# Smaller first loads, more warming products and a halved last store in a two-layer encoder trunk

## The chip, the cores and the metric

The kernel runs on one core of one Trainium2 chip. The metric is device time in microseconds (us), the median of several runs. All work is in float32, carried by the tensor engine in its float32r form (high and low parts, see below). Engine names are those of the profile: PE is the tensor engine's product, PEld its weight load, DVE the vector engine, ACT the scalar engine, POOL GpSimd, SP the sync engine. A small q behind a name is that engine's instruction queue, where its loads and stores are issued.

## What is computed

Two layers of one encoder trunk over 256 tokens of 2048 channels. Cut to what matters here:

```python
def hybrid_layer(x, cos, sin, norm_g, w_in, ...):
    h = rmsnorm(x, norm_g)
    proj = h @ w_in                      # 2048 x 13376
    (c_a, c_glu, c_gate, q_down, kv_down, k_pe, m_gate, g_conv, g_mla) = split(proj)
    y_conv = conv_branch(c_a, c_glu, c_gate, ...) @ w_proj_conv
    y_mla = mla_branch(q_down, kv_down, k_pe, m_gate, cos, sin, ...) @ w_proj_mla
    y = sigmoid(g_conv) * y_conv + sigmoid(g_mla) * y_mla
    return x + y @ w_out

def reference(x, positions, ...):
    cos, sin = rope_tables(positions, x.dtype)
    for l in range(2):
        x = hybrid_layer(x, cos, sin, ...)
    return x
```

## The kernel before

**The stream of weights.** All weights are cut into blocks of at most 512 columns, a block into pieces of four K tiles (a K tile is 128 rows of the weight), and a piece into two splits of two K tiles. `load` brings a piece into one of three `raw` buffers with one load on SP's queue. `split` makes the high part `hi` on ACT (L175) and the low part `lo` on DVE (L176), into one of three buffers each. `product` then runs, for each split, each half t of the tokens and each of the split's K tiles, three products into one accumulator: high by `hi` (L211), high by `lo` (L212), low by `hi` (L213). That is 12 products in a split and 96 in a block of 16 K tiles. Splits are asked for two ahead of the products, loads two pieces ahead. Four accumulators `acc` make two blocks; a block's accumulators must be evacuated before the block after next begins.

**The order.** A scheduler orders each engine's instructions by a simulated timeline; the priority is the order of the program. An instruction passed to `keep_in_program_order` is held behind the instruction that was traced last on its engine before it.

**The start.** Block 0 is the first of three blocks of the down projections (384, 384 and 320 columns). Its stationary operands are the transposed input times the norm's gain, split as well: `h_hi` on ACT (L326) and `h_lo` on DVE (L327), 16 K tiles of 256 tokens each. `x_in` is loaded in chunks of 2, 2, 4, 4 and 4 K tiles on SP, with the first pieces of weights between them; piece 0 is loaded in two halves. Ahead of these SP loads the `gains`. While the loads are on their way nine products of zeros (L258) run on PE. The constants of the rotary tables, `invf` (one row, broadcast to all partitions) and `pos`, are loaded on POOL's queue, and some 60 small DVE instructions (L275 to L303) and four Sin on ACT make the tables from them. `load_consts` loads two sets of constants on SP during block 1.

**The norm's factor.** `first_sums` loads the untransposed input in eight parts on SP (L333), ACT sums their squares (L335), and `sum_x` makes `rinv_x` from them on DVE. `down_evac` (L362) needs it to evacuate block 0.

**The end.** `wout_evac` adds an accumulator to the residual (L759) and, in the last layer, stores the 128x512 result on SP's queue (L761), 256 KB each. The last block's two halves of tokens are the last two of these.

Of the kernel before, what the change touches and what calls it, by code (L numbers as in the profile page):

```python
# [11 lines left out]
F32 = mybir.dt.float32  # L12
# [7 lines left out]
P = 128  # L20
T = 2
SEQ = 256
D = 2048
NCT = D // P
DEPTH = 2
# [15 lines left out]

# Columns of the input projection, by part.
O_A, O_GLU, O_CGATE = 0, D, 2 * D
# [4 lines left out]

# Widths of the blocks that the down projections are cut into.
DOWN_BLOCKS = ((0, 384), (384, 384), (768, 320))  # L50

# Per-partition constants of a layer: where each begins.
C_CB, C_LG, C_LB, C_QG, C_KG, C_CW = 0, 16, 32, 48, 49, 50
C_N = C_CW + NCT * CONV_W
R_QA, R_KVA, R_QR, R_KR, R_N = 0, LORA, 2 * LORA, 2 * LORA + ROPE, 2 * LORA + 2 * ROPE

KG = 4  # K tiles in one load of weights
KS = 2  # K tiles in one split of weights
N_WARM = 9  # products of zeros that warm the tensor engine's clock
SUMS_AFTER = 1  # splits before the loads for the first sums of squares  # L60

# [3 lines left out]
def revolution_pieces():  # L65
    """1 / (2 pi) as a sum of 12-bit pieces, each exact in float32."""
    from fractions import Fraction

    pi = Fraction(
        "3.14159265358979323846264338327950288419716939937510582097494459230781640628620899"  # L70
    )
    rest, out = 1 / (2 * pi), []
    for i in range(REVOLUTION_PIECES):
        unit = Fraction(1, 1 << (12 * (i + 1)))
        n = int(rest / unit)
        out.append(float(n * unit))
        rest -= n * unit
    return out


def blocks_of_layer():
    """(stream, K tiles, columns) of each block of a layer, in each stream's order."""
    s = {"win": [], "wuq": [], "wukv": [], "wpc": [], "wpm": [], "wo": []}
    for _, n in DOWN_BLOCKS:
        s["win"].append(n)
    s["win"] += [512] * 24
    s["wuq"] = [2 * QK] * NPAIR
    s["wukv"] = [2 * (NOPE + VH)] * NPAIR
    for w in ("wpc", "wpm", "wo"):
        s[w] = [512] * 4  # L90
    return s
# [3 lines left out]
def trunk(ctx: ExitStack, tc: tile.TileContext, xT, x, g_in, pos, win, wuq, wukv, wpc, wpm, wo, cst, rows, invf, out):  # L95
    nc = tc.nc
    pool = lambda name, bufs, **kw: ctx.enter_context(tc.tile_pool(name=name, bufs=bufs, **kw))
    const = pool("const", 1)
# [15 lines left out]

# [1 line left out]
    streams = {"win": (win, 16), "wuq": (wuq, 4), "wukv": (wukv, 4), "wpc": (wpc, 16), "wpm": (wpm, 16), "wo": (wo, 16)}  # L116
# [17 lines left out]

# [1 line left out]
    plans = []  # L136
# [17 lines left out]
    def load(i):  # L154
        if i >= len(pieces) or i in loaded:
            return
        ap, n = pieces[i]
        t = raw_p.tile([P, KG, n], F32, tag="raw", name=f"raw{i}")
        step = KS if i == 0 else KG
        for k in range(0, KG, step):  # L160
            if i == 0:
                load_x(k // step)
            nc.sync.dma_start(t[:, k : k + step, :], ap[:, k : k + step, :])
        loaded[i] = t

    def split(i):
        if i >= len(splits) or i in done:
            return
        piece, h, n = splits[i]
        load(piece)  # L170
        r = loaded[piece][:, h * KS : (h + 1) * KS, :]
        hi = split_p.tile([P, KS, n], F32R, tag="hi", name=f"hi{i}")
        lo = split_p.tile([P, KS, n], F32R, tag="lo", name=f"lo{i}")
        with tc.high_priority(offset=SPLIT_SOONER):
            nc.scalar.copy(hi, r)  # L175
            nc.vector.tensor_sub(lo, r, hi.bitcast(F32))  # L176
        done[i] = hi, lo
        for a in range(1, LOAD_AHEAD + 1):
            load(piece + a)

# [1 line left out]
    attn, fill = deque(), deque()  # L182
# [39 lines left out]

# [1 line left out]
    def rsqrt(y, ms):  # L224
        """y = ms ** -0.5, both float32 views of the same shape."""
        shape = list(ms.shape)
# [14 lines left out]

# [1 line left out]
    ident = const.tile([P, P], F32, name="ident")  # L243
    make_identity(nc, ident)
    ones = const.tile([P, P], F32, name="ones")
    nc.vector.memset(ones, 1.0 / D)

    cos2 = const.tile([P, T, 2, HALF], F32, name="cos2")
    sin2 = const.tile([P, T, 2, HALF], F32, name="sin2")

    # The engines' first steps while the first loads are on their way: the tensor engine's clock
    # and the table of the activations.
    zeros = work.tile([P, 512], F32R, tag="junk", name="zeros")
    nc.vector.memset(zeros.bitcast(F32), 0.0)
    nc.scalar.copy(sin2[:, 0, 0, :], ones[:, :HALF])
    warm = tp_p.tile([P, 512], F32, tag="tp", name="warm")
    for i in range(N_WARM):
        nc.tensor.matmul(warm, zeros[:, :P], zeros, start=i == 0, stop=i == N_WARM - 1)  # L258

    gains = const.tile([P, DEPTH, NCT], F32, name="gains")  # L260
    nc.sync.dma_start(gains, g_in)
    x_in = big.tile([P, NCT, SEQ], F32, tag="big", name="x_in")
    x_chunks = [(0, 2), (2, 4), (4, 8), (8, 12), (12, 16)]

    def load_x(i):
        a, b = x_chunks[i]
        nc.sync.dma_start(x_in[:, a:b, :], xT[:, a:b, :])

    def rope_tables():
        invf_t = const.tile([P, HALF], F32, name="invf_t")  # L270
        nc.gpsimd.dma_start(invf_t, invf.partition_broadcast(P))
        pos_t = const.tile([P, T], I32, name="pos_t")
        nc.gpsimd.dma_start(pos_t, pos)
        posf = const.tile([P, T], F32, name="posf")
# [13 lines left out]
        def reduce_to(dst, src, scale):  # L288
            """dst = src * scale less the nearest whole number (src * scale is exact)."""
            nc.vector.tensor_scalar(whole, src, scale, big_half, op0=ALU.mult, op1=ALU.add)  # L290
            nc.vector.tensor_scalar(whole, whole, -big_half, None, op0=ALU.add)
            nc.vector.scalar_tensor_tensor(dst, src, scale, whole, op0=ALU.mult, op1=ALU.subtract)
# [21 lines left out]

# [1 line left out]
    h_hi = big.tile([P, NCT, SEQ], F32R, tag="big", name="h_hi")  # L316
    h_lo = big.tile([P, NCT, SEQ], F32R, tag="big", name="h_lo")
    load(0)
    for i in range(2, len(x_chunks)):
        load_x(i)  # L320
        if i < len(x_chunks) - 1:
            load(i - 1)
    consts = [const.tile([P, C_N], F32, name=f"cst{l}") for l in range(DEPTH)]
# [12 lines left out]

# [1 line left out]
    for l in range(DEPTH):  # L338
# [3 lines left out]

        # -- down projections --
        down_row = big.tile([P, T * DOWN + R_N], F32, tag="big", name=f"down{l}")
# [19 lines left out]
        def down_after(down=down, qkc=qkc, ss_d=ss_d, r_d=r_d, kpe=kpe, ccq=ccq, ssq_t=ssq_t, gqk=gqk, row=row, C=C):  # L364
# [24 lines left out]

            # The shared rotary key, gained and rotated.  # L390
            gained(ccq, cos2, R_KR)
# [11 lines left out]

        # -- attention --
        # Transposed queries and keys of a pair of heads: the parts without a rotary key (high and low
        # of q, of k), then the rotary parts, where head 0 has [q high; q low], [k high; k high] and
        # [k low; 0] on the two halves of the partitions and head 1 the halves swapped.
        qk_t = big.tile([P, 14 * SEQ], F32R, tag="big", name=f"qk_t{l}")
# [46 lines left out]
        def attention(b, pair_of=pair_of, ss_d=ss_d, kpe=kpe, ccq=ccq, ssq_t=ssq_t, gqk=gqk, nope_t=nope_t, rope_t=rope_t, rope_k=rope_k, rope_l=rope_l, o_sb=o_sb, pt_h=pt_h, pt_l=pt_l, rinv=rinv):  # L455
# [56 lines left out]
            def scores():  # L512
                s0 = s_p.tile([P, 2, 2, P], F32, tag="s0", name="s0")
                s1 = s_p.tile([P, 2, SEQ], F32, tag="s1", name="s1")
                # The first block of queries: the keys' high and low parts side by side.
                for h in range(2):
# [19 lines left out]
                for s, nkeys in ((s0, P), (s1, SEQ)):  # L536
                    # The first chunk of a block of queries doesn't see the block's second chunk of keys.
                    nc.vector.memset(s[:CHUNK, :, nkeys - CHUNK :], MASKED)
# [53 lines left out]

        # -- convolution --
        us, vs = {}, {}
# [89 lines left out]

        # -- gates, projections, output --
        keep = {}

        def four(evac_src, dst_hi, dst_lo, c, t):
            """Turn a [tokens, 512 channels] tile and split it into the stationary operand's parts."""
            tp = tp_p.tile([P, 4, P], F32, tag="tp", name="tp4")  # L690
# [64 lines left out]
        def wout_evac(c, t, ps, keep=keep, l=l, last_layer=last_layer):  # L755
            blk = slice(c * 512, (c + 1) * 512)
            xt = wide_p.tile([P, 512], F32, tag="w", name="xres")
            nc.gpsimd.dma_start(xt, (x if l == 0 else x1_dram)[t, :, blk])
            nc.vector.tensor_add(xt, ps, xt)  # L759
            if last_layer:  # L760
                nc.sync.dma_start(out[t, :, blk], xt)  # L761
                return
# [17 lines left out]

        # -- run --
        for kind, i, pl in planned:
# [51 lines left out]

# [1 line left out]
def _blocked(w, widths):  # L836
    """[K, N] -> per block of columns: [K / 512][128][4][columns], flat."""
    k, at, out = w.shape[0] // (KG * P), 0, []
    for n in widths:
        b = w[:, at : at + n].reshape(k, KG, P, n).transpose(0, 2, 1, 3)  # L840
        out.append(b.reshape(-1))
        at += n
    return np.concatenate(out)
# [60 lines left out]
```

## Time and profile before

| | us |
|---|---|
| median of 3 runs | 1961.72 |
| lowest and highest of the 3 | 1961.68 to 1962.62 |
| span of the profiled execution | 1960.8 |
| PE busy in the span | 1951.5 |
| DVE busy | 1546.2 |
| ACT busy | 1107.4 |

The median of the runs stands 0.92 us above the span of the profiled execution, which runs from its first to its last instruction. Busy times are shares of the span; several engines are busy at the same time. Products are pipelined, so the duration of one is longer than the distance from one to the next.

### The profile page before, as it was taken

The page shows a single profiled execution, that of the slowest core. Times are in us where ns is not written, and L with a number is a line of the kernel's source. Part 1 is how long each engine was busy: PE and PEld are TensorE (multiplying, and loading weights), DVE is VectorE, ACT ScalarE, POOL GpSimd, SP SyncE. Part 2 cuts the span into 40 slices and gives each one's busy share as a digit, 9 for nine tenths or more (in the row PEclk, how much of TensorE's full clock was granted, in tenths as well). Part 3 has the DMA queues.
Part 4 walks back from the last instruction along what each step waited for, and adds up shares of the span by engine and source line. Part 5 has one row for each costly group of instructions (what it writes and reads, how often), then busy time and mean ns, then how long its engine had stood idle before and what let it go on. Part 6 is the DMA issues. An engine that isn't in the chain of part 4 may idle for free.

```text
span 1960.8 us, 25239 instructions
## 1 busy us (share of the span) xinstructions
PE 1951.5 (100%) x9333; PEld 1649.7 (84%) x9333; DVE 1546.2 (79%) x2738; ACT 1107.4 (56%) x1761; POOL 17.6 (1%) x50
## 2 busy tenths in 40 slices
PE   9999999999999999999999999999999999999999
PEld 8888888888888888888898888888888888888887
DVE  7788987889998787555557888878899987875554
ACT  6668767665443456444556686676654434464443
POOL 0000000000000000000000000000000000000000
PEclk9999999999999999999999999999999999999999
DMA  7654444445555555456665544444455555554564
GB/s 287 209 178 160 172 164 160 164 169 177 195 194 191 194 187 193 178 197 216 204 217 187 186 154 166 176 150 170 170 182 192 197 192 194 186 188 177 199 225 150
DMA packets 55532, 365.17 MB, mean 186 GB/s; under 512 B 6496, under 2 KB 6512, under 8 KB 16496
## 3 DMA queue, kind: packets, MB, share of 16 engines
q1 hardware_dynamic: 53424, 357.25, 51.7%
q0 software_dynamic: 1984, 6.31, 0.9%
q8 instruction: 73, 1.20, 0.2%
q14 instruction: 51, 0.42, 0.1%
HBM read 359.34 MB, written 4.19 MB: 185 GB/s over the span
## 4 chain that ended last, share of the span: by engine, by line
PE 98%; DVE 1%; DMA 0%; ACT 0%; issue 0%; SPq 0%
PE acc L212 31%; PE acc L213 31%; PE acc L211 31%; PE o_ps L580 1%; PE s L534 1%; PE tp_qk L489 1%; DVE v_t L670 0%; PE tp_rope L502 0%; PE tp_mg L706 0%; PE tp L692 0%; PE tp_u L607 0%; DMA raw<-in_win 0%; PE tp_cg L735 0%; DVE lo L176 0%; PE s L520 0%; PE s L518 0%
## 5 line engine op out<-in xcount | busy, mean ns | idle before, releaser
L175 ACT CAST hi<-raw 128x1024 fp32r<-128x1024 f32 (+2 forms) x688 | 704.9, 1025 | 747.9 <-PE acc L213 508.9
L176 DVE TENSOR_TENSOR lo<-raw,hi 128x1024 fp32r<-128x1024 f32 (+2 forms) x688 | 816.0, 1188 | 324.2 <-ACT hi L175 321.1
L627 DVE SCALAR_TENSOR_TENSOR v_t<-u_t,cst,v_t 128x256 f32<-128x256 f32 x960 | 412.3, 478 | 1.1
L212 PE MATMUL acc<-lo,h_hi 128*128 128x512 f32 (+2 forms) x864 | 334.0, 387 | 0.2 <-DVE lo L176 0.2
L212 PE MATMUL acc<-lo,hT 128*128 128x512 f32 (+2 forms) x864 | 333.2, 386 | 0.2 <-DVE lo L176 0.2
L213 PE MATMUL acc<-hi,h_lo 128*128 128x512 f32 (+2 forms) x864 | 332.8, 385 | 0.0
L213 PE MATMUL acc<-hi,hT 128*128 128x512 f32 (+2 forms) x864 | 332.1, 385 | 0.0
L211 PE MATMUL acc<-hi,h_hi 128*128 128x512 f32 (+2 forms) x864 | 305.3, 386 | 2.9 <-ACT hi L175 2.9
L211 PE MATMUL acc<-hi,hT 128*128 128x512 f32 (+2 forms) x864 | 303.8, 384 | 0.0
L211 PEld LDWEIGHTS acc<-hi,h_hi 128*128 128x128 f32 x864 | 162.1, 189 | 32.9 <-ACT hi L175 3.6
L212 PEld LDWEIGHTS acc<-lo,h_hi 128*128 128x128 f32 x864 | 163.0, 189 | 30.0 <-DVE lo L176 1.3
L212 PEld LDWEIGHTS acc<-lo,hT 128*128 128x128 f32 x864 | 162.3, 188 | 29.5 <-DVE lo L176 0.8
L213 PEld LDWEIGHTS acc<-hi,h_lo 128*128 128x128 f32 x864 | 162.9, 189 | 28.5
L213 PEld LDWEIGHTS acc<-hi,hT 128*128 128x128 f32 x864 | 162.3, 188 | 28.5
L211 PEld LDWEIGHTS acc<-hi,hT 128*128 128x128 f32 x864 | 161.4, 188 | 29.5
L212 PE MATMUL acc<-lo,ycT 128*128 128x512 f32 x256 | 100.5, 392 | 0.0
L212 PE MATMUL acc<-lo,yT 128*128 128x512 f32 x256 | 99.9, 390 | 0.0
L213 PE MATMUL acc<-hi,ycT 128*128 128x512 f32 x256 | 99.9, 390 | 0.0
L213 PE MATMUL acc<-hi,yT 128*128 128x512 f32 x256 | 99.7, 389 | 0.0
L213 PE MATMUL acc<-hi,oT 128*128 128x512 f32 x256 | 99.6, 389 | 0.0
L212 PE MATMUL acc<-lo,oT 128*128 128x512 f32 x256 | 99.6, 389 | 0.0
L212 PE MATMUL acc<-lo,qkc 128*128 128x384 f32 (+1 forms) x256 | 94.2, 368 | 0.0
(207 smaller groups left out, 2270.5 us busy)
## 6 DMA issues: line engine op xcount, KB each, us to landing
raw<-in_win SPq DMA_DIRECT2D x192, 1024.0 KB, 4.8
raw<-in_wpm SPq DMA_DIRECT2D x32, 1024.0 KB, 4.8
raw<-in_wpc SPq DMA_DIRECT2D x32, 1024.0 KB, 4.7
raw<-in_wo SPq DMA_DIRECT2D x32, 1024.0 KB, 4.9
raw<-in_wukv SPq DMA_DIRECT2D x16, 1024.0 KB, 4.8
raw<-in_wuq SPq DMA_DIRECT2D x16, 768.0 KB, 4.2
raw<-in_win SPq DMA_DIRECT2D x15, 768.0 KB, 5.7
raw<-in_win SPq DMA_DIRECT2D x8, 640.0 KB, 3.9
```

The lines of the kernel that those rows point to most:

```text
L175: nc.scalar.copy(hi, r)
L176: nc.vector.tensor_sub(lo, r, hi.bitcast(F32))
L211: nc.tensor.matmul(pts[t][:, :n], sh, hi[:, kk, :], start=first, stop=False)
L212: nc.tensor.matmul(pts[t][:, :n], sh, lo[:, kk, :], start=False, stop=False)
L213: nc.tensor.matmul(pts[t][:, :n], sl, hi[:, kk, :], start=False, stop=last)
L489: nc.tensor.transpose(tp[:, h, t * P : (t + 1) * P], src[:, t, h, :NOPE], ident)
L534: nc.tensor.matmul(s1[:, h, :], qa, ka, start=n == 0, stop=n == len(terms) - 1)
L580: nc.tensor.matmul(o_ps[:, h, kt * P :], v[j][:, kt, h, :], pt[i][:, h, queries], start=n == 0, stop=n == len(todo) - 1,)
L627: nc.vector.scalar_tensor_tensor(dst, src, w, dst, op0=ALU.mult, op1=ALU.add)
```

## The change

Five edits, all at the start or the end of the program:

- Piece 0 is loaded in steps of 1, 1 and 2 K tiles, and the chunks of `x_in` become 1, 1, 2, 4, 4 and 4 K tiles, one chunk before each step. Split 0 is made K tile by K tile.
- The `gains` are loaded on ACT's queue instead of ahead of `x_in` on SP's.
- Eleven warming products instead of nine, and DVE clears `zeros` before it fills `ones`.
- `invf` and `pos` are loaded on SP's queue and held behind the load that was traced last there (piece 6), no longer on POOL's. The tables' arithmetic is the same.
- In the last block of columns of the last layer each 128x512 sum and store become two of 128x256, one stored on SP's queue, one on ACT's.

Comments and docstrings are left out too. The core of the diff:

```diff
-N_WARM = 9  # products of zeros that warm the tensor engine's clock
+FIRST_STEPS = ((0, 1), (1, 2), (2, 4))
+N_WARM = 11
...
-        step = KS if i == 0 else KG
-        for k in range(0, KG, step):
+        for j, (a, b) in enumerate(FIRST_STEPS if i == 0 else ((0, KG),)):
             if i == 0:
-                load_x(k // step)
-            nc.sync.dma_start(t[:, k : k + step, :], ap[:, k : k + step, :])
+                load_x(j)
+            nc.sync.dma_start(t[:, a:b, :], ap[:, a:b, :])
...
+        step = 1 if i == 0 else KS
         with tc.high_priority(offset=SPLIT_SOONER):
-            nc.scalar.copy(hi, r)
-            nc.vector.tensor_sub(lo, r, hi.bitcast(F32))
+            for a in range(0, KS, step):
+                s = slice(a, a + step)
+                nc.scalar.copy(hi[:, s], r[:, s])
+                nc.vector.tensor_sub(lo[:, s], r[:, s], hi[:, s].bitcast(F32))
...
-    nc.vector.memset(ones, 1.0 / D)
...
+    x_chunks = [(0, 1), (1, 2), (2, 4), (4, 8), (8, 12), (12, 16)]
...
+    nc.scalar.dma_start(gains, g_in)
     zeros = work.tile([P, 512], F32R, tag="junk", name="zeros")
     nc.vector.memset(zeros.bitcast(F32), 0.0)
+    nc.vector.memset(ones, 1.0 / D)
...
-    nc.sync.dma_start(gains, g_in)
...
-        nc.gpsimd.dma_start(invf_t, invf.partition_broadcast(P))
+        tc.keep_in_program_order(nc.sync.dma_start(invf_t, invf.partition_broadcast(P)))
         pos_t = const.tile([P, T], I32, name="pos_t")
-        nc.gpsimd.dma_start(pos_t, pos)
+        tc.keep_in_program_order(nc.sync.dma_start(pos_t, pos))
...
-    for i in range(2, len(x_chunks)):
+    for i in range(3, len(x_chunks)):
         load_x(i)
         if i < len(x_chunks) - 1:
-            load(i - 1)
+            load(i - 2)
...
-            nc.vector.tensor_add(xt, ps, xt)
+            last = last_layer and c == 3
+            for a, engine in ((0, nc.sync), (256, nc.scalar)) if last else ():
+                s = slice(a, a + 256)
+                nc.vector.tensor_add(xt[:, s], ps[:, s], xt[:, s])
+                engine.dma_start(out[t, :, c * 512 + a : c * 512 + a + 256], xt[:, s])
+            if not last:
+                nc.vector.tensor_add(xt, ps, xt)
             if last_layer:
-                nc.sync.dma_start(out[t, :, blk], xt)
+                if c < 3:
+                    nc.sync.dma_start(out[t, :, blk], xt)
                 return
```

## Rows read from the trace of the kernel before

**Rows 1.** The page's first line.

```profile
span 1960.8 us, 25239 instructions
```

**Rows 2.** Timeline of the start: start, duration, engine, instruction, idle before.

```profile
0.74 0.39 SPq L261 DMA_DIRECT2D gains<-in_g  x1
...
0.83 0.17 DVE L246 MEMSET ones<- 128x128 f32 x1 [0.83 <-PEq L893]
1.05 0.48 DVE L254 MEMSET zeros<- 128x512 f32 x1
1.18 0.42 SPq L267 DMA_DIRECT2D x_in<-in_xT  x1
1.28 0.67 POOL L271 DMA_DIRECT2D invf_t<-in_invf  x1 [0.34 <-issue]
...
1.59 4.21 PE L258 MATMUL warm<-zeros 128*128 128x512 f32 x9 [1.59 <-DVE zeros L254]
...
3.54 0.43 SPq L163 DMA_DIRECT2D raw<-in_win  x1
...
7.97 0.17 DVE L275 CAST posf<-pos_t 128x2 f32<-128x2 int32 x1 [2.16 <-DMA pos_t<-in_pos]
```

**Rows 3.** The chain that ended last, its pieces at the start: start, length, what.

```profile
8.67 1.01 PE acc L211 x2
...
12.91 0.32 PE acc L213
...
13.84 0.17 PE acc L212
```

**Rows 4.** Busy time by stretch; the last two columns are DMA share and GB/s.

```profile
3.50:6.50 3.00, 2.30 (x6) 1.29 (x4) 0.88 (x2) 0.91 (x2) 0.34 (x5) 1.00 0.62 117
6.50:12.50 6.00, 3.83 (x11) 3.34 (x12) 4.02 (x13) 4.18 (x8) 0.00 (x0) 1.00 1.04 419
```

**Rows 5.** DMA issues: tile, queue, size, us from issue to landing (raw: piece 1).

```profile
gains<-in_g SPq DMA_DIRECT2D x1, 16.0 KB, 1.6
invf_t<-in_invf POOLq DMA_DIRECT2D x1, 16.0 KB, 5.4
...
x_in<-in_xT SPq DMA_DIRECT2D x1, 256.0 KB, 3.1
...
raw<-in_win SPq DMA_DIRECT2D x1, 768.0 KB, 9.1
...
out<-xres SPq DMA_DIRECT2D x2, 256.0 KB, 2.3
```

**Rows 6.** Groups by shape, first 60 us: busy, mean ns of one, idle before.

```profile
L176 DVE TENSOR_TENSOR lo<-raw,hi 128x768 fp32r<-128x768 f32 x16 | 15.3, 955 | 2.4 <-ACT hi L175 2.3
L175 ACT CAST hi<-raw 128x768 fp32r<-128x768 f32 x16 | 13.1, 831 | 8.4 <-PE acc L213 4.4 <-DMA raw<-in_win 2.7 <-DVE whole L291 1.2
...
L176 DVE TENSOR_TENSOR lo<-raw,hi 128x640 fp32r<-128x640 f32 x8 | 6.6, 825 | 6.7 <-ACT hi L175 6.7
L175 ACT CAST hi<-raw 128x640 fp32r<-128x640 f32 x8 | 5.8, 728 | 5.6 <-PE acc L213 5.6
...
L291 DVE TENSOR_SCALAR whole<-whole 128x64 f32<-128x64 f32 x14 | 2.7, 193 | 0.2
```

**Rows 7.** Timeline around the rotary tables, block 0's evacuation and block 2's start.

```profile
24.47 0.42 SPq L163 DMA_DIRECT2D raw<-in_win  x1
...
26.88 0.96 DVE L176 TENSOR_TENSOR lo<-raw,hi 128x768 fp32r<-128x768 f32 x1 [0.87 <-ACT hi L175]
...
42.42 0.16 DVE L235 SCALAR_TENSOR_TENSOR rinv_x<-rsq_t,rinv_x 128x2 f32<-128x2 f32 x1
...
43.28 1.51 ACT L362 ACTIVATE down<-acc,rinv_x 128x384 f32<-128x384 f32 x3
...
44.53 0.31 PE L211 MATMUL acc<-hi,h_hi 128*128 128x320 f32 x1
```

**Rows 8.** Timeline of the end.

```profile
1956.39 0.69 DVE L759 TENSOR_TENSOR xres<-acc,xres 128x512 f32<-128x512 f32 x1 [0.44 <-PE acc L213]
```

More of the change, by code (lines that the diff above doesn't have):

```diff
@@ L245, in trunk, with load_x @@
     ones = const.tile([P, P], F32, name="ones")
-    nc.vector.memset(ones, 1.0 / D)
     cos2 = const.tile([P, T, 2, HALF], F32, name="cos2")
     sin2 = const.tile([P, T, 2, HALF], F32, name="sin2")
+    x_in = big.tile([P, NCT, SEQ], F32, tag="big", name="x_in")
+    x_chunks = [(0, 1), (1, 2), (2, 4), (4, 8), (8, 12), (12, 16)]
+    def load_x(i):
+        a, b = x_chunks[i]
+        nc.sync.dma_start(x_in[:, a:b, :], xT[:, a:b, :])
+    gains = const.tile([P, DEPTH, NCT], F32, name="gains")
+    nc.scalar.dma_start(gains, g_in)
     zeros = work.tile([P, 512], F32R, tag="junk", name="zeros")
     nc.vector.memset(zeros.bitcast(F32), 0.0)
+    nc.vector.memset(ones, 1.0 / D)
     nc.scalar.copy(sin2[:, 0, 0, :], ones[:, :HALF])
@@ L258, in trunk @@
         nc.tensor.matmul(warm, zeros[:, :P], zeros, start=i == 0, stop=i == N_WARM - 1)
-    gains = const.tile([P, DEPTH, NCT], F32, name="gains")
-    nc.sync.dma_start(gains, g_in)
[L262 to L267, printed above, removed]
     def rope_tables():
         invf_t = const.tile([P, HALF], F32, name="invf_t")
-        nc.gpsimd.dma_start(invf_t, invf.partition_broadcast(P))
+        tc.keep_in_program_order(nc.sync.dma_start(invf_t, invf.partition_broadcast(P)))
         pos_t = const.tile([P, T], I32, name="pos_t")
-        nc.gpsimd.dma_start(pos_t, pos)
+        tc.keep_in_program_order(nc.sync.dma_start(pos_t, pos))
         posf = const.tile([P, T], F32, name="posf")
```

## The prediction

> **What bounds the kernel now.** I read the page first. Its span is 1960.8 us [rows 1], and the table above gives PE 1951.5 us of it. Only 9.3 us remain in which PE doesn't run, so whatever the change can win lies there, or in products at less than full speed. The list of waits and the chain show where they are. At the start PE first waits for the zeros, runs nine warming products to 1.59 + 4.21 = 5.80, and then stands still until 8.67 [rows 2, 3]. From there the chain is PE products one behind another to the end, so a start that is earlier by some time, or faster, is an end that is earlier by that much, as long as nothing else comes to hold PE.
>
> The pieces of the chain also show a clock. The products of 384 columns follow one another by 0.32 us up to 13.8 and by 0.17 from there [rows 3]: 1.2 columns a nanosecond is the lower of the tensor engine's two levels (1.2 GHz), 2.2 is the upper one (2.4 GHz). The clock column reads 1.00 in both stretches [rows 4], so here the distances tell more than the column. From 8.67 to 13.84 there are 14 products at the lower level. From 13.84 to the first product of block 2 at 44.53 there are 2 x 96 - 14 = 178, that is 0.1724 us each [rows 3, 7]: no waits are hidden in them. I therefore write PE's progress as the time at which it would have started had it run at full speed throughout: 13.84 - 14 x 0.1724 = **11.43 us**. The kernel's gain at the start is 11.43 less the same figure of the changed kernel.
>
> At the end, the last sum starts on DVE at 1956.39 and takes 0.69 [rows 8]; the store that follows lands 2.3 us after its issue [rows 5].
>
> **Start: three limits, the latest decides.**
>
> *Warming.* DVE clears zeros first instead of second, so they are ready 1.05 - 0.83 = 0.22 us sooner (the second clearing starts where the first did). The warming products then start at 1.37. Two more of 512 columns at 1.2 per ns cost 0.85, so they end at 1.37 + 4.21 + 0.85 = 6.43 [rows 2]. PE works in order, so no real product starts before about 6.4, however early the data are.
>
> *Clock.* In the trace the rise came 5.0 us after products were resumed at 8.67, and the nine before the idle time brought none. If the run is unbroken from 1.37, the same 5.0 us give 6.4: no real product at the lower level. The bounds are no product and again 14 products at the lower level, which cost 14 x (0.32 - 0.1724) = 2.07 us. I take 0, since idle time is what separates the two runs of products in the trace. The Trainium skill, TensorE: Matmul & The Clock Gate (The HAM clock gate), says that the lower level is the default, that activity lifts it, and that the number of products at it varies between runs of one kernel. That agrees with the 14 here; its variation no run here shows.
>
> *Data.* K tiles 0 and 1 come early: x's first load moves from 1.18 to 0.74, where the gains stood [rows 2]. Split 0 in two parts costs more: from 768 to 640 columns ACT saves 0.103 and DVE 0.130 us [rows 6], so 384 columns cost 0.831 - 0.309 = 0.52 on ACT and 0.955 - 0.390 = 0.565 on DVE, twice each, or 0.21 and 0.18 more than whole. The warming products cover this; without them it would add at most 0.4. The load that is late next is piece 1, which holds K tiles 4 to 7 whole and feeds split 2. It was issued at 3.54 and landed 9.1 us later, at 12.64 [rows 2, 5]. From x's first issue at 1.18 that is 11.46 us. K tiles 0 to 7 of x and weights are 2.62 MB, 6.26 us at the 419 GB/s of the next stretch [rows 4]; 5.20 us are something else. Between 3.5 and 6.5 the rate was only 117 GB/s, worth 3.0 x (1 - 117/419) = 2.16 us [rows 4]. That is when POOL's two loads were in flight: the 16 KB of invf took 5.4 us from 1.28, where the 16 KB of the gains took 1.6 on SP [rows 2, 5]. I read the first as crowding out the weights. The change takes both from the start, so 2.16 goes and 3.04 is left. The fixed part of a lone load is between 1.6 (gains) and 3.04; I take 2.3. Two more loads ahead of piece 1 cost between nothing and two issues, which follow one another by (3.54 - 1.18) / 5 = 0.47 [rows 2]; I take 0.4. Piece 1 then lands at 0.74 + 6.26 + 2.3 + 0.4 = 9.7 (bounds 0.74 + 6.26 + 1.6 = 8.6, and 12.2 if nothing but the earlier issue counts). With hi (0.83) and lo (0.955) behind it and 0.04 between, lo of split 2 is there at 11.55. The 26th product is the first to need it: 11.55 - 25 x 0.1724 = **7.24**. That is later than 6.43, so the data decide.
>
> The gain at the start is 11.43 - 7.24 = **4.19 us**. The bounds are 11.43 - 6.43 = 5.0 (data in time) and, with piece 1 at 12.2, 11.43 - (14.04 - 4.31) = 1.7.
>
> A rule speaks against the small loads: the Trainium skill, DMA: Bandwidth & Descriptors (Rules for kernel authors, and its fit in Anatomy of one DMA), wants 1 MiB a load and gives 2.0 us fixed per load plus bytes at 436 GB/s. By it 128 KB would take an estimated 2.3 us against 2.6 for 256 KB, and two more loads paid in turn would eat 4 us, leaving no gain. The trace's loads overlap: they are issued 0.47 us apart and land together at 419 GB/s, so I give the rule a small share, under the third rival.
>
> **Rotary tables.** Their two loads move from POOL's queue to SP's, behind piece 6 at 24.47 [rows 7], by then some 4.2 us earlier. What is queued behind them on SP, the two sets of constants and the next pieces, moves back by two issues of about 0.42. lo of split 9 starts at 26.88 [rows 7], PE comes to it at 11.43 + 108 x 0.1724 = 30.05, so 2.2 us of slack cover this. The DVE work of some 60 x 0.2 = 12 us [rows 6] leaves the first 20 us, which helps split 2, and falls after it; their first use that PE comes to is after block 2. I cost it at nothing.
>
> **Block 0's evacuation.** It starts at 43.28, three in 1.51 us, so the first ends at 43.8; block 2 wants that accumulator at 44.53 [rows 7]. The slack is 0.7. With PE 4.2 earlier, rinv_x must come 3.5 earlier. The squares before it stand between ACT's splits, which PE paces, so I expect them to move along; nothing is taken off, 3.5 us is the price if they don't.
>
> **End.** A half sum costs 0.69 - 256 x 0.00102 (DVE's slope above) = 0.43; two cost 0.86. The last store is issued 0.17 later and carries 128 KB less, 0.31 us at 419 GB/s: **0.14 us** gained. Bounds: 0.31 gained (halves at half price) and 0.38 lost (halves at full price).
>
> **Sum.** 4.19 + 0.14 = 4.33 us: a span of 1956.5. The median of the runs stands 0.92 above the span, so 1961.72 - 4.33 = **1957.4 us**. A measurement of this kernel can tell about 0.2%, 3.9 us, from no change: the bar is 1957.8.
>
> **The rivals.**
>
> 1. *The data are no limit* (chance 0.18). Piece 1 lands by 8.9, PE starts at 6.43 and never waits: 5.0 + 0.14, 1956.6. For it: the 16 KB of the gains landed in 1.6. Against it: 3.04 us of the first loads' time have no explanation but a slow beginning.
> 2. *The clock doesn't rise in the warming* (0.08). Fourteen products at 1.2 GHz from 6.43 give 8.5: 2.9 + 0.14, 1958.7. For it: nine products of zeros raised nothing.
> 3. *The loads stay slow at the start* (0.10). Then POOL's loads weren't the cause, or the small loads eat what they freed: 1.7 + 0.14, 1959.9.
> 4. *Block 0's evacuation holds PE* (0.07). rinv_x stays at 42.42 and block 2 starts no earlier than 0.7 before 44.53: 0.7 + 0.14, 1960.9.
> 5. *The other side: DVE waits for pos* (0.07). In order, DVE stops at L275 until pos has landed; it did so for 2.16 us [rows 2]. Now pos comes behind piece 6: issued near 20.7, landing at 26 or later with the 5.4 us of invf. If the schedule puts L275 early, the splits' lo stand behind it. The loss is the wait less 2.2 us of slack; it turns the result from a wait of 2.2 + 4.3 = 6.5 on. A wait of 10 costs 7.8: 1965.2.
>
> **How the numbers follow.** The forecast has the remaining 0.50, with a range of its own from 1956.9 to 1958.4; about two thirds of that lie under 1957.8. Faster: 0.18 + 0.34 = 0.52. Slower: the last rival, 0.07. Same: 0.41. The range reaches from 1956.0, under the first rival, to 1960.2, which takes in the second and third and leaves out the last two.
>
> **What the profile will show.** If I am right: POOL issues no load at the start; the rate between 3.5 and 6.5 us is far above 117 GB/s; the first real product starts near 6.4 and goes on by 0.17 us; a short wait of PE for lo of split 2; block 2 starts near 40.3 with evacuation before it; the last store lands about 0.1 earlier after PE's end. I am wrong if PE's products from 6.4 on are 0.32 apart, if piece 1 lands after 11, or if PE waits before block 2 or behind a DVE that stands at L275.

## The result, and the profile after

The changed kernel takes 1965.30 us (median of 21 runs, 1964.45 to 1967.24), the kernel before 1962.12 (21 runs, 1961.68 to 1963.53). The ratio is 1.0017, 95% interval 1.0011 to 1.0023: 3.2 us slower, where 4.3 us faster was forecast. That is less than the 0.2% which the prediction took as the least that can be told from no change, but the interval leaves out 1, and the time lies outside the predicted range, on the other side of zero.

The page's first line of the changed kernel answers to [rows 1]. This execution took 1965.15 us, 1.85 more than its span.

```profile
span 1963.3 us, 25255 instructions
```

The timeline of the start, which answers to [rows 2, 3] (start, duration, engine, instruction, idle time before):

```profile
0.74 0.38 SPq L259 DMA_DIRECT2D x_in<-in_xT  x1
...
1.45 4.62 PE L269 MATMUL warm<-zeros 128*128 128x512 f32 x11 [1.45 <-DVE zeros L264]
...
4.01 0.43 SPq L163 DMA_DIRECT2D raw<-in_win  x1
...
5.91 0.52 PE L214 MATMUL acc<-hi,h_hi 128*128 128x384 f32 x2
6.28 0.34 PE L215 MATMUL acc<-lo,h_hi 128*128 128x384 f32 x1
6.45 0.34 PE L216 MATMUL acc<-hi,h_lo 128*128 128x384 f32 x1
...
8.94 0.62 PE L214 MATMUL acc<-hi,h_hi 128*128 128x384 f32 x2 [0.43 <-ACT hi L178]
9.94 0.44 PE L215 MATMUL acc<-lo,h_hi 128*128 128x384 f32 x1 [0.37 <-DVE lo L179]
```

The real products begin at 5.91 instead of 8.67 and stand 0.17 us apart from 6.28 on; short waits for hi and lo follow. The loads of this stretch, by DMA issues (tile, queue, size, us to landing; the raw load is piece 1), answer to [rows 5]:

```profile
raw<-in_win SPq DMA_DIRECT2D x1, 768.0 KB, 7.2
```

Piece 1 lands at 4.01 + 7.2 = 11.2. The busy times by stretch answer to [rows 4] and go on to the end of block 1. The columns are the stretch, its length, the busy time of PE, PEld, DVE, ACT and POOL, the granted clock, DMA share and GB/s:

```profile
3.50:6.50 3.00, 3.00 (x12) 2.44 (x11) 1.52 (x3) 1.32 (x4) 0.00 (x0) 1.00 0.92 182
6.50:12.50 6.00, 5.01 (x24) 3.57 (x22) 4.46 (x9) 5.09 (x10) 0.00 (x0) 1.00 1.02 416
42.00:44.00 2.00, 0.21 (x2) 0.00 (x0) 1.81 (x11) 0.72 (x1) 0.00 (x0) 1.00 0.59 195
44.00:46.00 2.00, 0.34 (x2) 0.35 (x3) 1.90 (x14) 0.98 (x3) 0.00 (x0) 1.00 0.34 138
46.00:47.00 1.00, 1.00 (x7) 1.00 (x6) 0.86 (x5) 1.00 (x4) 0.00 (x0) 0.69 0.09 16
47.00:49.00 2.00, 2.00 (x10) 2.00 (x9) 1.73 (x10) 1.91 (x4) 0.00 (x0) 0.50 0.00 0
49.00:50.00 1.00, 1.00 (x6) 1.00 (x6) 0.92 (x5) 0.40 (x2) 0.00 (x0) 0.60 0.00 0
50.00:51.00 1.00, 1.00 (x9) 1.00 (x8) 0.50 (x3) 0.40 (x2) 0.00 (x0) 1.00 0.00 0
```

PE is nearly empty from 42 to 46 and then gets half its clock until nearly 50. What it waits for is in the timeline around block 2's start, which answers to [rows 7]:

```profile
36.01 0.84 ACT L178 CAST hi<-raw 128x768 fp32r<-128x768 f32 x1 [0.37 <-DVE whole L292]
36.75 0.63 ACT L337 ACTIVATE junk<-xres 128x512 f32<-128x512 f32 x1
...
38.58 0.15 DVE L314 TENSOR_REDUCE totx<-ss_x 128x2 f32<-128x8 f32 x1
...
38.91 0.82 DVE L179 TENSOR_TENSOR lo<-raw,hi 128x640 fp32r<-128x640 f32 x1
...
40.93 0.83 DVE L179 TENSOR_TENSOR lo<-raw,hi 128x640 fp32r<-128x640 f32 x1 [0.59 <-ACT hi L178]
...
41.87 0.34 PE L216 MATMUL acc<-hi,h_lo 128*128 128x384 f32 x1
...
42.25 0.72 ACT L178 CAST hi<-raw 128x640 fp32r<-128x640 f32 x1 [1.35 <-DVE whole L292]
...
43.01 0.83 DVE L179 TENSOR_TENSOR lo<-raw,hi 128x640 fp32r<-128x640 f32 x1 [0.19 <-ACT hi L178]
...
44.84 0.15 DVE L238 SCALAR_TENSOR_TENSOR rinv_x<-rsq_t,rinv_x 128x2 f32<-128x2 f32 x1
...
45.02 1.99 ACT L364 ACTIVATE down<-acc,rinv_x 128x384 f32<-128x384 f32 x4 [2.05 <-DVE rinv_x L238]
45.66 0.41 PE L214 MATMUL acc<-hi,h_hi 128*128 128x320 f32 x1 [3.44 <-ACT down L364]
...
46.35 0.42 PE L215 MATMUL acc<-lo,h_hi 128*128 128x320 f32 x1
46.57 0.47 PE L216 MATMUL acc<-hi,h_lo 128*128 128x320 f32 x1
46.84 0.47 PE L214 MATMUL acc<-hi,h_hi 128*128 128x320 f32 x1
```

Block 1's last product starts at 41.87, so block 2 could start at 42.04. It starts at 45.66, because block 0's evacuation (L364) waits for rinv_x, whose last step ends at 44.99 instead of 42.58. The same stretch of the kernel before, beside [rows 7]:

```profile
35.82 0.63 ACT L335 ACTIVATE junk<-xres 128x512 f32<-128x512 f32 x1
...
37.29 0.15 DVE L312 TENSOR_REDUCE totx<-ss_x 128x2 f32<-128x8 f32 x1
...
41.50 0.82 DVE L176 TENSOR_TENSOR lo<-raw,hi 128x640 fp32r<-128x640 f32 x1
...
42.65 0.73 ACT L175 CAST hi<-raw 128x640 fp32r<-128x640 f32 x1 [1.35 <-PE acc L213]
```

Two things came later. The last of the eight squares starts at 36.75 instead of 35.82, and the sums are complete at 38.58 instead of 37.29, though PE is 2.49 us earlier. And between the factor's first step (totx) and its last stand the lo of block 2's first three splits (640 columns wide; splits 16, 17 and 18), two of them after a wait for their hi. Before, the lo of split 16 (41.50) and two of block 1 (768 columns) stood there, and none waited. From totx to the factor it is 6.41 us instead of 5.29.

The hi at 42.25 is that of split 18. There are three hi buffers; its own was last read by block 1's last product, which ends at 41.87 + 0.34 = 42.21, 0.04 before. The view names a DVE instruction of the tables as what ended the wait, because it ended last (42.06 + 0.19 = 42.25), but hi reads nothing of it. Before, hi of split 17 (42.65) stands as far behind the product that freed its buffer (42.28 + 0.33 = 42.61), and there the view names PE.

Once PE runs again, its products are 0.15 apart, then 0.27 to 49.77.

The end, which answers to [rows 8]:

```profile
1958.80 0.39 PE L216 MATMUL acc<-hi,yT 128*128 128x512 f32 x1
1958.89 1.47 ACTq L765 DMA_DIRECT2D out<-xres  x2
1959.23 0.75 DVE L764 TENSOR_TENSOR xres<-acc,xres 128x256 f32<-128x256 f32 x2 [0.38 <-PE acc L216]
```

**The account of the two profiled executions.** Before, block 2 started at 44.53 and never waited; now it could at 42.04: 2.49 us gained. The wait takes back 45.66 - 42.04 = 3.62. From 45.66 to 49.94 there are 18 distances, 4.28 us instead of 18 x 0.147 = 2.64: 1.64 lost. Together 2.77 lost; PE's last product starts at 1958.80 instead of 1955.96, 2.84 later. From there to the end of the span it is 4.50 us instead of 4.84. That leaves 2.50, the difference of the spans. The medians lie 3.2 apart: the profiled execution of the kernel before was among the slower half of its runs (about 1962.6), so 0.7 of the difference is not in these two traces.

### The profile page after: what moved, and what is told of

It is laid out like the page before. It is cut to its first block, busy times and chain, and to the rows that moved or that the text cites. A ratio compares the mean times of both kernels' runs of the same rounds, so it can differ in the third digit from the quotient of the medians.

```text
span 1963.3 us, 25255 instructions
## 1 busy us (share of the span) xinstructions
PE 1952.5 (99%) x9335; PEld 1649.8 (84%) x9335; DVE 1547.9 (79%) x2741; ACT 1108.0 (56%) x1762; POOL 16.4 (1%) x48
## 3 DMA queue, kind: packets, MB, share of 16 engines
HBM read 359.34 MB, written 4.19 MB: 185 GB/s over the span
## 4 chain that ended last, share of the span: by engine, by line
PE 97%; DVE 1%; DMA 0%; ACT 0%; issue 0%; SPq 0%; DVEq 0%
PE acc L215 31%; PE acc L216 30%; PE acc L214 30%; PE o_ps L582 1%; PE s L536 1%; PE tp_qk L491 1%; DVE lo L179 1%; DVE v_t L672 0%; DMA raw<-in_win 0%; PE tp_u L609 0%; PE tp L694 0%; PE tp_mg L708 0%; PE tp_rope L504 0%; ACT hi L178 0%; PE tp_cg L737 0%; PE s L522 0%
## 5 line engine op out<-in xcount | busy, mean ns | idle before, releaser
L178 ACT CAST hi<-raw 128x1024 fp32r<-128x1024 f32 (+3 forms) x689 | 705.1, 1024 | 748.2 <-PE acc L216 506.7
L179 DVE TENSOR_TENSOR lo<-raw,hi 128x1024 fp32r<-128x1024 f32 (+3 forms) x689 | 815.7, 1186 | 327.4 <-ACT hi L178 324.6
```

The source lines that it names most:

```text
L178: nc.scalar.copy(hi[:, s], r[:, s])
L179: nc.vector.tensor_sub(lo[:, s], r[:, s], hi[:, s].bitcast(F32))
```

## The experiments

Each changes the changed kernel, unless it says otherwise. The kernel before ran beside them at medians of 1962.12 to 1962.76, so times of different rounds can be compared to some 0.6 us.

**The rotary loads back on POOL.**

```diff
-        tc.keep_in_program_order(nc.sync.dma_start(invf_t, invf.partition_broadcast(P)))
+        nc.gpsimd.dma_start(invf_t, invf.partition_broadcast(P))
```

(and pos alike)

> The changed kernel with the loads of invf and pos on POOL's queue again, all else as changed. Theory A (the later tables hold up rinv_x: their loads stand among the loads for the sums of squares, their 60 DVE instructions among the steps of sum_x): rinv_x comes before 42, PE doesn't wait for L364 before block 2, no drop of the clock there; the start loses part of its 2.5 us gain, since POOL's loads are back in the first 7 us (piece 1 lands near 12 and not 11.2). Time 1961.0 to 1962.5. Theory B (the sums of squares can't come earlier at all, and any earlier PE must wait for them): block 2 starts no earlier than 44.5, PE waits as long as it is early, time 1962.7 to 1965.

1961.55 us (1961.23 to 1961.79; ratio 0.9997, 0.9988 to 1.0006). The wait is gone: block 2 starts at 43.75, behind an evacuation that begins at 42.50. But the start is 1.7 us worse than the changed kernel's 42.04. So the move causes the loss, and also most of the gain at the start.

**The tables' arithmetic a block later.**

```diff
-                if l == 0 and i == 0:
+                if l == 0 and i == 1:
                     rope_tables()
```

> The changed kernel with the tables asked for after block 1 and not after block 0. Theory A1 (the tables' DVE instructions between the steps of sum_x make its chain long, 38.58 to 44.99): the chain takes under 4 us, rinv_x is there by 42.5, PE waits under 1 us before block 2 and its clock stays up: 1965.3 - 3.0 - 1.6 = 1960.7, at most 1962. Theory A2 (the loads for the sums land late because other loads stand before them, so sum_x starts late): the first step of sum_x moves earlier too, by 1 us or more, since invf and pos no longer stand before the last of these loads. Theory C (the splits' lo between the steps, which wait for PE, make the chain long): the chain stays over 5 us, PE waits over 2.5 us, 1964 to 1965.5.

1964.56 us (1963.12 to 1965.49; ratio 1.0012, 1.0003 to 1.0021). All but three of the tables' steps are gone from between the factor's steps, yet PE still waits 2.80 us, and its products are 0.27 apart behind that. Table arithmetic isn't the main cause; the three lo still stand there, the last at 43.16.

**Nothing on ACT's queue.** The gains and the second half stores on SP.

```diff
-    nc.scalar.dma_start(gains, g_in)
+    nc.sync.dma_start(gains, g_in)
...
-            for a, engine in ((0, nc.sync), (256, nc.scalar)) if last else ():
+            for a, engine in ((0, nc.sync), (256, nc.sync)) if last else ():
```

> The changed kernel with the gains first on SP's queue again and both halves of the last stores on SP's queue: nothing is issued on ACT's queue. Theory D (a program that uses ACT's queue pays about 0.9 us around its span): time less span falls from 1.8 to 0.9 us; the span changes by 0.4 later loads at the start, which the wait before block 2 hides, and 0.1 to 0.3 at the end: 1964.3 to 1964.9. Rival (the 0.9 us around the span has another source): time less span stays at 1.8, time 1965 to 1966.

1965.94 us (ratio 1.0020, 1.0011 to 1.0029). ACT's queue costs nothing outside the span: the time stands 1.7 to 1.9 us above the span in every execution, here, of the changed kernel and of the kernel before. The start is 0.68 later than the changed kernel's, the wait is 3.45 again: it does not shrink when PE comes later.

**Products into the wait.** 16 products of 512 columns, traced ahead of block 2.

```diff
+                if l == 0 and i == 2:
+                    busy = tp_p.tile([P, 512], F32, tag="tp", name="busy")
+                    for k in range(N_BUSY):
+                        nc.tensor.matmul(
+                            busy, h_hi[:, 0, :P], h_hi[:, 0:2, :].rearrange("p k s -> p (k s)"),
+                            start=k == 0, stop=k == N_BUSY - 1,
+                        )
```

> The changed kernel with 16 extra products of 512 columns (into an unused accumulator) on PE between blocks 1 and 2, some 3.5 us at the upper level. They add no result. Theory E (the wait of 3.4 us itself costs 3.4, and the fall of the clock behind it another 1.6): rinv_x comes at the same time, block 2 starts at 45.7 as before, but its products follow one another by 0.147 us from the first: 1965.3 - 1.6 = 1963.7. Rival (the products after the wait are at the lower level for another reason, such as DVE and ACT being busy): products still 0.27 apart for 3 us, 1965.3.

1961.24 us (1960.63 to 1961.49). It didn't test what it was meant to: the schedule put twelve of the extra products at 6.95 to 9.94, into split 0, and four at 14.13, and with them came another order, in which rinv_x was done at 38.3 and block 2 started at 43.83 without a wait.

**The same, held in place.**

```diff
-                        nc.tensor.matmul(
+                        tc.keep_in_program_order(nc.tensor.matmul(
```

> The changed kernel with 16 more products of 512 columns, held behind the last product of block 1, so that PE works through most of its 3.4 us wait (16 x 0.215 = 3.4 us). Their result isn't used. If the idle time is what brings PE's clock down: block 2 starts near 45.7 as before, but its products stand 0.17 apart from the first on, and the time is 1965.3 - 1.6 = 1963.7. If the clock falls for another reason: 13 products 0.27 apart stay, 1965.3.

1964.04 us (1963.62 to 1964.76). Its timeline and two of its stretches:

```profile
41.79 3.83 PE L807 MATMUL busy<-h_hi 128*128 128x512 f32 x16
45.45 0.37 PE L215 MATMUL acc<-hi,h_hi 128*128 128x320 f32 x1
45.66 0.30 PE L216 MATMUL acc<-lo,h_hi 128*128 128x320 f32 x1
```

```profile
44.00:46.00 2.00, 2.00 (x12) 1.59 (x11) 1.86 (x13) 1.23 (x3) 0.00 (x0) 1.00 0.25 100
46.00:48.00 2.00, 2.00 (x16) 2.00 (x14) 1.74 (x10) 1.38 (x4) 0.00 (x0) 1.00 0.01 3
```

Block 2 starts nearly as late as in the changed kernel (45.45), but the clock stays at 1.00 and 1.3 us come back: PE's idle time is what brought the clock down.

**The factor from a constant.** Block 0 is then scaled by it instead of the true factor; loads and squares stay.

```diff
-        nc.vector.reduce_sum(tot, ss_x, axis=AX.X)
+        nc.vector.memset(tot, float(D))
```

> The changed kernel, but rinv_x is made from a constant instead of from the sums of squares (their loads and squares stay; what is left out is that block 0 is scaled by the true factor). Theory A, the whole loss is that rinv_x comes late: no PE wait before block 2, which starts near 42.0 us instead of 45.66; no products 0.27 apart behind it; time 1965.3 - 3.6 - 1.6 = 1960.1 us. Rival B, the evacuation is held by ACT's own order (squares and splits), not by the factor: a wait of over 2 us stays, 1963.5 or more. Rival C, the clock falls in that stretch whatever PE waits: no wait, but 13 products 0.27 apart, 1961.7.

1959.97 us (1959.41 to 1961.22; ratio 0.9988, 0.9979 to 0.9997). Block 2 starts at 42.27, without a wait, and no products are 0.27 apart. The late factor is the whole loss.

**One edit alone, on the kernel before**: first the rotary loads on SP.

```diff
-        nc.gpsimd.dma_start(invf_t, invf.partition_broadcast(P))
+        tc.keep_in_program_order(nc.sync.dma_start(invf_t, invf.partition_broadcast(P)))
...
-        nc.gpsimd.dma_start(pos_t, pos)
+        tc.keep_in_program_order(nc.sync.dma_start(pos_t, pos))
```

> The kernel before with one edit, the rotary loads on SP behind piece 6. Theory A (the move makes the factor late and frees the start): the stretch from 3.5 to 6.5 us moves more than 117 GB/s and block 1 ends 1 to 2 us earlier than 44.5, rinv_x comes near 45 instead of 42.4, PE waits before block 2 and its clock falls; 1962.8 to 1964.5. Rival (the move alone delays nothing that PE waits for): no wait, 1960.4 to 1961.8.

1965.27 us (1964.87 to 1966.33; ratio 1.0017, 1.0008 to 1.0026): this edit alone gives the changed kernel's time. The time lies 0.8 above the range expected; the mechanism is the expected one. Its timeline and its first stretch:

```profile
42.11 0.34 PE L213 MATMUL acc<-hi,h_lo 128*128 128x384 f32 x1
45.90 0.41 PE L211 MATMUL acc<-hi,h_hi 128*128 128x320 f32 x1 [3.45 <-ACT down L362]
```

```profile
3.50:6.50 3.00, 2.36 (x7) 1.42 (x6) 1.02 (x3) 1.91 (x4) 0.00 (x0) 1.00 0.98 337
```

Block 2 could start at 42.28, 2.25 us earlier than before; the other three edits at the start add 0.24 to that.

Then the halved last sum and store, again on the kernel before:

```diff
+            last = last_layer and c == 3
+            for a, engine in ((0, nc.sync), (256, nc.scalar)) if last else ():
```

> The kernel before with one edit, the halved last sum and store. By the trace of the changed kernel the time from PE's end to the end of the span is 0.3 us shorter: 1961.8, with the products before it unchanged. Rival (the second queue costs outside the span what it gains inside): 1962.1 or more.

1962.09 us beside 1962.29 (ratio 0.9999, 0.9991 to 1.0008): a gain of 0.2 or none.

**Why is the factor late?** Two places were left: the last two loads for the sums, which now stand on SP behind invf, pos and the constants, and the lo in DVE's order. First the loads:

```diff
-SUMS_AFTER = 1
+SUMS_AFTER = 0
```

> The changed kernel with SUMS_AFTER 0 alone, a one-character edit: the loads for the sums begin one split sooner, all eight are then issued ahead of the rotary loads and constants. If the place of the last two sums' loads behind those four is the cause, this alone removes the wait: 1959.9 to 1960.5. If the loads that now come earlier hold up piece 3 or 4, PE waits for weights between 15 and 25 us instead: 1961 or more.

1960.60 us (1959.45 to 1961.19; ratio 0.9990, 0.9982 to 0.9999). One character removes the wait before block 2: the sums are complete at 35.28, and the last step of the factor comes before block 2's first lo. Loads and DVE's order changed together, so this doesn't separate them. The next two do: they leave every load in its place and only put a lo behind the factor, by writing two of its columns from rinv_x first.

```diff
                 nc.scalar.copy(hi[:, s], r[:, s])
+                if i == 17:
+                    nc.vector.tensor_copy(lo[:, 0, 0:T], rinv_x)
```

> The changed kernel with one more DVE instruction: before lo of split 17 (the second of block 2) two of its columns are written from rinv_x and then overwritten, so that this lo and the next stand behind the factor's last step in DVE's order instead of between its steps. The loads, the squares and their order stay; totx comes at 38.6 as before. If DVE's order makes the factor late: about 18 steps of 0.12 from 40.3 on, rinv_x near 42.7, evacuation behind hi of split 18 at 43.0, block 2 at 43.6, a wait of 1.4 us instead of 3.44 and no fall of the clock: 1965.3 - 2.0 - 1.6 = 1961.7 us. Rival (the late loads and squares alone make it late): the wait stays above 3 us, 1965 or more.

1961.61 us (1961.06 to 1962.31). Its timeline:

```profile
38.69 0.15 DVE L316 TENSOR_REDUCE totx<-ss_x 128x2 f32<-128x8 f32 x1
...
42.62 0.15 DVE L240 SCALAR_TENSOR_TENSOR rinv_x<-rsq_t,rinv_x 128x2 f32<-128x2 f32 x1
...
42.98 1.99 ACT L366 ACTIVATE down<-acc,rinv_x 128x384 f32<-128x384 f32 x4
43.10 0.83 DVE L181 TENSOR_TENSOR lo<-raw,hi 128x640 fp32r<-128x640 f32 x1
...
43.60 0.42 PE L216 MATMUL acc<-hi,h_hi 128*128 128x320 f32 x1 [1.30 <-ACT down L366]
```

The sums are complete at the same time as in the changed kernel (38.69, 38.58), but the factor is there 2.2 us sooner, PE waits 1.30 instead of 3.44, and the clock stays up.

For split 18 alone:

```diff
+                if i == 18:
+                    nc.vector.tensor_copy(lo[:, 0, 0:T], rinv_x)
```

> The same for lo of split 18 alone, which DVE comes to last ahead of the factor and which waits for hi of split 18, and that for the buffer which PE frees with its last products of block 1. If the factor hangs on PE's own progress through this lo: rinv_x comes 0.9 us earlier (0.19 of waiting and 0.74 of work), the wait is 2.5 us, the time 1964.4, or 1962.8 if the clock doesn't fall after so short a wait. Rival: no change, 3.4 us and 1965.3.

1963.25 us (1962.30 to 1964.95). With split 18's lo alone moved the wait is 2.49, as worked out:

```profile
45.40 0.42 PE L216 MATMUL acc<-hi,h_hi 128*128 128x320 f32 x1 [2.49 <-ACT down L366]
```

In the profiled execution no stretch behind it has a clock below 1.00, and the median lies nearer the lower of the two times expected. Three of the eleven executions took 1964.50 to 1964.95, the other eight at most 1963.33. The three show a mean clock of 0.999 over the span, as one of the eight does, and seven show 1.000; that the clock fell in the three is likely, but no trace shows it.

**The rotary loads on ACT's queue.**

```diff
-        tc.keep_in_program_order(nc.sync.dma_start(invf_t, invf.partition_broadcast(P)))
+        tc.keep_in_program_order(nc.scalar.dma_start(invf_t, invf.partition_broadcast(P)))
```

> The changed kernel with the rotary loads on ACT's queue at the same place of the program; the schedule then puts them and the whole arithmetic of the tables behind block 0's evacuation, while two of the sums' loads still stand behind the two sets of constants on SP. If both the two rotary issues on SP (0.85 us) and the tables' steps between the factor's steps (1 us) make the factor late: rinv_x near 43, a wait of 1 to 1.8 us, 1961 to 1962.5. If only the constants' place matters: a wait of 3 us stays, 1964.5 or more.

1967.35 us (1965.11 to 1969.27; ratio 1.0024, 1.0015 to 1.0034), slowest of all. The first wait was 2.36: split 18's lo (42.74) still stood ahead of the factor's last step (43.48), but no steps of the tables. What wasn't expected is on DVE:

```profile
43.48 0.15 DVE L238 SCALAR_TENSOR_TENSOR rinv_x<-rsq_t,rinv_x 128x2 f32<-128x2 f32 x1
48.07 0.17 DVE L277 CAST posf<-pos_t 128x2 f32<-128x2 int32 x1 [4.43 <-DMA pos_t<-in_pos]
```

The loads came behind the evacuation, DVE stood for them for 4.43 us with block 2's lo behind it, and PE waited 3.18 us for a lo at 53.32. That is the fifth rival's mechanism, in a kernel that wasn't the one forecast.

**The sums first, with the new first steps and with the old ones.** SUMS_AFTER 0, the rotary loads held behind the last sums' load, the constants a block later.

```diff
+        if (t, c) == (T - 1, 3):
+            rope_loads()
...
-                elif i == 1:
+                elif i == 2:
                     load_consts()
```

> The changed kernel with the sums' loads first: they begin one split sooner (SUMS_AFTER 0), the rotary loads are held behind the last of them, and the two sets of constants are loaded a block later. If late loads for the last sums are what made the factor late: rinv_x is there before 41, PE doesn't wait before block 2, 1959.9 us as with the constant factor (1959.97). Rival (the factor's own steps on DVE, with the tables' between them, take the time however early the sums are): PE still waits 1 us or more and its clock falls, 1962 to 1964.

1960.15 us (1959.27 to 1961.02; ratio 0.9988, 0.9979 to 0.9997); no wait, block 2 at 42.95. The same with x's chunks, piece 0 and split 0 in the steps of the kernel before:

```diff
-FIRST_STEPS = ((0, 1), (1, 2), (2, 4))
+FIRST_STEPS = ((0, 2), (2, 4))
...
-    x_chunks = [(0, 1), (1, 2), (2, 4), (4, 8), (8, 12), (12, 16)]
+    x_chunks = [(0, 2), (2, 4), (4, 8), (8, 12), (12, 16)]
```

> The same as the run with the sums' loads first, but piece 0, x's chunks and split 0 in the old steps of two K tiles. By my prediction the small steps cost 0.4 us of issue and make the first split ready sooner, which the warming products cover: 0.2 to 0.5 faster than with the small steps. By the rate between 3.5 and 6.5 us (337 GB/s with the old steps and no POOL loads, 182 with the small ones) piece 1 comes sooner and PE waits less: 1 us faster. If the small steps do help: 0.2 to 1 slower.

1959.00 us (1958.34 to 1959.36; ratio 0.9982, 0.9973 to 0.9991), the fastest of all and 3.3 us faster than the kernel before. Of its timeline, and its first stretch:

```profile
41.49 0.31 PE L214 MATMUL acc<-hi,h_hi 128*128 128x320 f32 x1
```

```profile
3.50:6.50 3.00, 2.84 (x10) 1.81 (x8) 1.42 (x3) 1.63 (x3) 0.00 (x0) 1.00 1.03 351
```

Against its twin with small steps it starts block 2 at 41.49 instead of 42.95 and moves 351 GB/s between 3.5 and 6.5 us instead of 230. The small first steps, loads and split together, cost 1.15 us; they don't help.

## Why the prediction was wrong

**The step that failed** is block 0's evacuation: "I expect them to move along; nothing is taken off". I had its slack (0.7) and what a standstill would cost (3.5). The squares didn't move along. The last of them stood behind hi of split 13 on ACT before and stands behind hi of split 15 now (36.01), so it starts 0.93 later while PE comes 2.49 earlier. Its load isn't what holds it: with the tables a block later that load landed 1.0 us sooner, and the square started at 36.74 all the same.

And I didn't look at what stands between totx and rinv_x on DVE. There the order is written once, by the scheduler, and DVE keeps to it. With the rotary loads on SP it has the lo of splits 17 and 18 ahead of the factor's last steps. The lo of split 18 waits for its hi, and that waits for a buffer that PE frees with block 1's last products. So the factor hangs on PE's own progress: from 42.04 on, 0.21 to the start of hi, 0.76 to that of lo, 0.74 to the next instruction on DVE (43.75), 1.24 for the ten that are left until the factor is there (44.99), six of them the tables', and 0.67 for the evacuation: 3.62. PE arriving earlier can't shorten that; it was 3.44, 3.45 and 3.45 in three kernels whose block 2 could have begun at different times (42.04, 42.28 and 42.72).

Taking the two lo out, with the sums as late as ever, left 1.30 of the 3.44 us of waiting and gave back 3.7 of the 5.3 us; the constant factor gave back all of it. The 1.30 that stay I put down to the late sums: in the three kernels with the sums' loads sooner there is no wait. Since the order on DVE changed there too, the share of the sums alone isn't measured.

**The rivals.** The fourth had the right place and the wrong price: it left rinv_x at 42.42, where it came at 44.84, and it didn't see that the wait lets the clock fall. 3.62 + 1.64 = 5.26 us stand against the 3.5 that I named. The clock's part is shown: products in place of the idle time kept it at 1.00 and gave back 1.3 us. The Trainium skill, TensorE: Matmul & The Clock Gate (HAM oscillation — how this bites in real kernels), describes this for waits on loads: such a wait sends the clock to the lower level, and the products behind it start there. The rows above agree, with a wait for an evacuation. The fifth rival's wait for pos didn't occur (the changed kernel has no wait of DVE for pos). That the other side of zero was reached by a different mechanism than the one I gave it shows how thin 0.07 was, and that its example of 1965.2 stands so near the 1965.30 measured is chance.

**Rotary tables at nothing.** Wrong by way of that order: alone, on the kernel before, this edit costs 3 us.

**Warming and clock**: right in the time, not shown in the cause. The first real product came at 5.91 (forecast 6.43), since the clock rose within the warming, and no later product of the start is 0.32 apart. But with the rotary loads moved alone, nine warming products from 1.60 to 5.75 were followed by real ones at 6.38 that were at the upper level too, so the two more aren't shown to be needed. One reading was wrong: 13.84 is a piece of the chain, and the fifteenth product starts at 13.67. The distance is then (44.53 - 13.67) / 178 = 0.1734 and the figure before 13.67 - 14 x 0.1734 = 11.24, so the forecast gain was some 0.15 too large from this alone.

**Data**: right mechanism, wrong size. Piece 1 landed at 11.2, not 9.7: from x's first issue 10.47 us, where I had 6.26 + 2.3 + 0.4. Without POOL's loads and with the old steps it is 3.54 + 8.0 - 1.18 = 10.4, against 11.46 before, so POOL's loads cost 1.1 us of it and not 2.16. Beside the small steps even that can't be told: with the rotary loads back on POOL piece 1 took 11.0 us from x's first issue, where the kernels with small steps and no load on POOL's queue took 10.2 to 11.6, and the rate from 3.5 to 6.5 us was the changed kernel's 182 GB/s. PE's start figure came to 42.04 - 192 x 0.1724 = 8.94 instead of 7.24, the gain at the start to 2.49 instead of 4.19 (inside its bounds of 1.7 and 5.0). I gave the small loads 0.4 us and the rule against them a small share. The twin runs put the small steps at 1.15. The Trainium skill, DMA: Bandwidth & Descriptors (Rules for kernel authors), which asks for large transfers, is right here in direction. Its fit, which the page gives for loads issued on GpSimd's queue, would make two loads paid in turn an estimated 4 us; for these loads on SP's queue that is too much.

**End**: 0.14 forecast, 0.34 in the profiled execution, 0.2 with an interval that includes none. Neither sign nor size can be told: with the whole store (the rotary loads alone) 4.39 us followed the last product's start, less than the 4.50 with halves. A half sum costs 0.37 (two in 0.75), not 0.43.

**Signs of being wrong**: two of those named came, piece 1 after 11 (11.2) and a wait of PE before block 2.

**Span and time**: the 0.92 compared the median with another execution's span. In one and the same execution it is 1.7 to 1.9, for both kernels, so the profiled execution before took about 1962.6. The gain was taken off the median, and this changes nothing in it.

What stays open: why the scheduler's order changes with the place of these two loads. It is a consequence of its simulated timeline; which of its times tips it wasn't tried.

## What to carry to other kernels

Before pricing an earlier start at "everything moves along", list for each value that gates PE what stands ahead of it in each engine's order, and ask whether any of that waits for PE itself: such a wait has a fixed length, and an earlier start only moves it. A wait of PE of some us costs more than its length when its clock falls behind it. When moving a load changes a schedule, compare the orders of all engines, not the queue it was moved on.

## What was not expected of the hardware

The same bytes in smaller first loads moved at 182 to 243 GB/s between 3.5 and 6.5 us, in larger ones at 337 and 351, with no load on POOL's queue in either. After the 3.44 us wait PE's first products, to 46.35, were still at the upper level's distance (0.15), and only then did some twelve come at the lower (0.27); after the wait of 2.49 none did in the profiled execution. The length of the wait alone doesn't tell whether the clock falls. In the profiled execution of the kernel with SUMS_AFTER 0 it fell at 11.5 after a wait of 1.53, with products in between, and cost part of that kernel's start:

```profile
10.07 0.62 PE L214 MATMUL acc<-hi,h_hi 128*128 128x384 f32 x2 [1.53 <-ACT hi L178]
```

```profile
11.50:14.90 3.40, 3.40 (x13) 3.40 (x12) 2.87 (x6) 3.21 (x7) 0.00 (x0) 0.50 1.03 421
```
